# Cached attention at three rates instead of one, six page tiles loaded early, and two more half-tiles in each prompt head

## The chip, the cores and the metric

The kernel runs on one core of one Trainium2 chip. The metric is the device time of one execution in microseconds (us); three runs of the kernel before gave 2747.08, 2751.02 and 2751.05 us, with a median of 2751.02 us. One further execution was profiled: it took 2750.36 us, with a span of 2748.6 us from its first to its last instruction.

## The reference, cut to what matters

One inference step of a decoder layer over 512 prompt tokens and 8 x 8 sample tokens; the sample tokens attend to 2048 cached positions each, kept in pages.

```python
h = rms_norm(x, g_mix) @ w_in             # columns: q | k | v | forget logits | conv value | conv gate
# prompt, per head: causal softmax with a cumulative log-forget bias
s = einsum('bqhd,bkhd->bhqk', qs, k) * scale + cq[..., :, None] - c[..., None, :]
p = softmax(where(causal, s, -inf));  o = einsum('bhqk,bkhd->bqhd', p, v)
# sample, per head: the same over the cached pages and the new tokens
k_past = cache_k[l][page_table].reshape(dec_b, past, N_HEADS, HEAD_DIM)     # v_past alike
s_past = einsum('bqhd,bkhd->bhqk', q, k_past) * scale + cn[..., :, None] + r_past[..., None, :]
# both: u = value * sigmoid(gate); causal depthwise conv of width 31; LayerNorm; swish
x = x + concat([rms_norm(attn), conv_y]) @ w_out
x = x + square(relu(rms_norm(x, g_mlp) @ w_up)) @ w_down
x = x + (pe @ w_ple) * sigmoid(rms_norm(x, g_ple) @ w_ple_gate)
```

## The kernel before, in words

All 576 token rows (512 prompt, 64 sample) go through every matrix multiplication together. An f32 product is made of three products of a high and a low part, so 128 columns of `w_in` (a **column tile**) cost 16 x 3 x 2 = 96 matmuls of 128 x 288. This case is about the first stage (`phase1`, the first 800 us), which makes 40 column tiles: four of q, and then 36 in the list `order`. After that come a short drain, the output projection (`w_out`) and the MLP (`phase2`), which the change doesn't touch.

**What sets the order.** Each engine runs its instructions in the order in which the program emits them. `gemm_tile` emits a column tile in eight pieces of 12 matmuls, called halves here after the function `half()` that is called behind each. `half()` places other work between the pieces: a step of the conv work (`side`), a step of the prompt attention (`att`), and, after every second half (a **pair**), perhaps a step of the cached attention (`decode`). A counter D["credit"] grows by DEC_RATE per pair, and a decode step is emitted when it reaches 1.

**The sections of `order`.** Places 0 to 10 are c0, q4, c1, q5, c2, q6, c3, q7, c4, k0, c5 (17 column tiles, as each c is a value and a gate tile); places 11 to 15 are v0, c6, k1, c7, v1 (7 tiles); places 16 to 27 are k2, v2 to k7, v7 (12 tiles). They are called sections 1, 2 and 3 in what follows, and have 68, 28 and 48 pairs.

**The cached attention.** `decode` makes 64 steps of scores (line L847, key tiles `k`) and, four steps later, of values (L878, value tiles `v`); a step uses two key tiles and two value tiles of 512 KB. A tile is two page gathers of 256 KB, whose row numbers are read from the page table: a DMA that SyncE (SP) issues at L821. Value tiles have four buffers and key tiles five, so a value tile is asked for two steps before its use, when its buffer has come free. Each fourth step the probabilities (`dp`) are transposed into the PSUM tile `T` (L837). The generator ends with the 69th call after its start. Weights of `w_in` (`wraw`, L112) are loaded by ScalarE's queue, 256 KB for four of the 16 blocks of a tile, and split into `whi` (ScalarE) and `wlo` (VectorE).

**A shared ring of semaphores.** The DMAs of SP and of ScalarE's queue take their completion semaphores from one ring of eight, in the order in which the program was laid out. A DMA waits until the one eight places before it in that ring has landed, whichever queue issued it.

**The prompt heads.** `prompt_head(h)` is queued in `att` when tile k of head h is done, and takes one step per half: scores (`S`, L730 to L733), transposes of the probabilities into `T` (L745), v transposed (L772), values (L753), and, after a norm on VectorE (`o`, L792), the transposes of the output (L798). Heads are worked off one after the other.

Of the kernel before, what the change touches and what calls it, by code (L numbers as in the profile page):

```python
# [9 lines left out]
F32 = mybir.dt.float32  # L10
# [8 lines left out]
NR = 576  # L19
# [5 lines left out]
NPG = 16  # L25
EPS = 1e-6
SCALE = 128.0 ** -0.5
NEG = -1.0e30
DEC_RATE = 0.495
DOWN_FIRST = (3, 3, 3, 4, 5, 6, 7, 8)  # L30
DOWN_PART = 7
RING = 8
# [110 lines left out]
class Kern:  # L143
# [99 lines left out]
    def phase1(self):  # L243
        tc, nc, a = self.tc, self.nc, self.a
# [1 line left out]
        P = lambda name, bufs, **k: es.enter_context(tc.tile_pool(name=name, bufs=bufs, **k))  # L246
        Q = lambda name, bufs: pes.enter_context(tc.tile_pool(name=name, bufs=bufs, space=PSUM))
        c1, sm = P("c1", 1), P("sm", 2)
        wes, xs, st, des = ExitStack(), ExitStack(), ExitStack(), ExitStack()
        xp = xs.enter_context(tc.tile_pool(name="xp", bufs=1, side="right"))  # L250
        w1 = wes.enter_context(tc.tile_pool(name="w1", bufs=3, side="right"))
        stp = self.stp = st.enter_context(tc.tile_pool(name="stp", bufs=1, reuse_waits="tile"))
        xqp = st.enter_context(tc.tile_pool(name="xq", bufs=1, reuse_waits="tile"))
        ps_, pt_, po_, pd_, pu = Q("ps", 1), Q("pt", 1), Q("po", 1), Q("pd", 1), Q("pu", 2)
        self.c1, self.w1, self.sm = c1, w1, sm
        S_ = lambda: ps_.tile([128, 512], F32, name="S", tag="S")
# [1 line left out]
        O_ = lambda: po_.tile([128, 512], F32, name="O", tag="O")  # L258
        D_ = lambda: pd_.tile([128, 512], F32, name="D", tag="D")
        U_ = lambda: pu.tile([128, 2, 512], F32, name="U", tag="U")  # L260
# [4 lines left out]
        order = [("q", 4), ("q", 5), ("q", 6), ("q", 7), ("k", 0), ("v", 0), ("k", 1), ("v", 1)]  # L265
        order = [x for c, q in enumerate(order) for x in (("c", c), q)]
# [11 lines left out]
        self.xh, self.xl = zip(*((xp.tile([128, 2, NR], F32R, name=f"xh{j}"), xp.tile([128, 2, NR], F32R, name=f"xl{j}"))  # L278
                                 for j in range(8)))
        rb = self.rb = c1.tile([128, NR], F32, name="rb")  # L280
        raw = [xqp.tile([128, 2, NR], F32, name=f"xraw{j}") for j in range(8)]
        self.ws.dma(1)
        for i in range(2):
            nc.sync.dma_start(raw[0][:, i, :], a["x"][:, i, :])
# [64 lines left out]


        side, att, fq = deque(), deque(), deque()
        D = {"credit": 0.0, "half": 0, "dec": None, "mid": None}

        def step(q):
            while q:
# [7 lines left out]
        def half():  # L363

            D["half"] += 1
            odd = D["half"] % 2
            self.flush_later()
            if D["dec"] is None:
                step(att)
                step(fq)  # L370
                return
            step(side)
            step(att)
            if odd:
                return
            D["credit"] += DEC_RATE
            if D["credit"] >= 1.0:
                D["credit"] -= 1.0
                if next(D["dec"], self) is self and D["mid"] is None:
                    des.close()  # L380
                    D["mid"] = mes.enter_context(tc.tile_pool(name="mid", bufs=2, reuse_waits="tile"))
                    self.ple_loads(D["mid"])
                    side.append(self.finish(1, D_, O_))

        def run(gen):
            for _ in gen:
                half()

        def norm():

            fp = self.f_proj(wf, bfb)
            for j in range(4, 8):
                square(j)
                yield
            acc = raw[0][:, 0, :]
            nc.vector.tensor_tensor(acc, acc, raw[0][:, 1, :], ALU.add)
            next(fp)
            yield
            yield
            rr = self.row_rsqrt(S_, sm, raw[3][:, 0, :], acc, rb, 2048.0)  # L400
            next(rr)
            next(fp)
            yield
            for _ in rr:
                yield
            for h in range(3):
                self.evac_q(h, l0[h], l0[h])
            yield from fp
# [14 lines left out]
        st.close()  # L423
        hd, cnp = P("hd", 1, reuse_waits="tile"), P("cnp", 1, reuse_waits="tile")
        self.hd, self.cnp = hd, cnp
        self.dec = des.enter_context(tc.tile_pool(name="dec", bufs=1, reuse_waits="tile"))
        dec = D["dec"] = self.decode()
        next(dec)

        for kind, i in order:  # L430
            if kind == "c":
                for j in range(2):
                    run(self.gemm_tile(lambda u: self.evac_cin(u, j, i, cb)))
                side.append(self.conv_tile(i, cb["ue"], cb["us"]))
                if i == 7:
                    side.append(self.conv_norm())
                    side.append(self.finish(0, S_, T_))
                continue
# [18 lines left out]
        n = 0  # L457
# [260 lines left out]
    def prompt_head(self, h, hb):  # L718

        nc, hd, sm = self.nc, self.hd, self.sm  # L720
        q, k = hb["q"], hb["k"]
        o = hd.tile([128, 4, 128], F32, name="o", tag="o")
# [40 lines left out]
        scores(1)  # L763
        for _ in range(2):
            yield
        while "v" not in hb:
            for _ in range(2):
                yield
        v = hb["v"]
        t = self.S_()  # L770
# [4 lines left out]
        t = self.T_()  # L775
# [16 lines left out]
                nc.vector.tensor_tensor(o, o, rs[:, :, None].broadcast_to([128, 4, 128]), ALU.mult)  # L792
            yield
        if not self.draining:
            yield
        t = self.T_()
        for qt in range(4):
            nc.tensor.transpose(t[:, qt * 128:qt * 128 + 128], o[:, qt, :], self.ident)  # L798
# [2 lines left out]
        nc.gpsimd.dma_start(self.am[h // 2][:, h % 2, :NPR], am)  # L801


    def decode(self):


        tc, nc, a, dec, sm = self.tc, self.nc, self.a, self.dec, self.sm
        V = nc.vector.tensor_tensor
        tiles = ([], [])

        def load(i, m):

            while len(tiles[i]) < min(m, 128):
                n = len(tiles[i])
                G, c, w, j = n // 32, n // 8 % 4, n // 2 % 4, n % 2
                t = dec.tile([128, 2, 4, 128], F32, name="kv"[i], tag="kv"[i] * 2, bufs=(5, 4)[i])
                for x in range(2):
                    b, pg = (w, 2 * j + x) if i == 0 else (2 * j + x, w)
                    e = (G % 2 * 4 + b) * NPG + c * 4 + pg
                    r = nc.sync.value_load(self.pti[0:1, e:e + 1])  # L820
                    nc.sync.dma_start(t[:, x].rearrange("p h c -> p (h c)"),  # L821
                                      a["cache_kv"][bass.ds(r, 1), G // 2, :, 512 * i:512 * i + 512].rearrange("o p c -> p (o c)"))
                tiles[i].append(t)

        s = o = mu = p = None
        al, ls = {}, {}
        one = lambda name: sm.tile([128, 1], F32, name=name, tag=name)
        for n in range(68):
# [11 lines left out]
            if n < 64:  # L840
                if w == 0:
                    s = self.D_()
                    nc.tensor.matmul(s, self.selU[:, G, :], self.R[:, c * 512:c * 512 + 512], start=True, stop=False)
                for i in range(2):
                    kt = tiles[0][2 * n + i]
                    for h in range(4):
                        nc.tensor.matmul(s[32 * h:32 * h + 32, i * 256:i * 256 + 256].rearrange("p (a b) -> p a b", a=2),  # L847
                                         self.q_of(G // 2 * 4 + h, G % 2 * 4 + w), kt[:, :, h, :],
                                         start=False, stop=(w == 3 and i == 1))
                if w == 3:  # L850
                    p = dec.tile([128, 512], F32, name="dp", tag="dp")
                    mx = one("dmx")
                    nc.vector.tensor_scalar(p, s, self.cns[:, G:G + 1], None, ALU.add, ALU.max, accum_out=mx)
                    new = self.mlu[:, 0, G:G + 1]
                    if c == 0:
                        nc.vector.tensor_copy(new, mx)
                        ls[sc] = self.mlu[:, 1, G:G + 1]
                    else:
                        al[sc], ls[sc] = one("dal"), one("dls")
                        V(mx, mx, new, ALU.max)  # L860
                        V(al[sc], new, mx, ALU.subtract)
                        nc.vector.tensor_copy(new, mx)
                    nm = one("dnm")
# [1018 lines left out]
```

## Time and profile before

| | |
|---|---|
| median of three runs | 2751.02 us |
| the profiled execution | 2750.36 us, span 2748.6 us |
| TensorE (PE) busy | 2669.2 us, 97% |
| VectorE (DVE), ScalarE (ACT), GpSimd (POOL) busy | 74%, 42%, 19% |
| weights' loads into TensorE (PEld) | 2571.8 us, 94% |
| HBM read, written | 441.47 MB, 90.96 MB |
| granted TensorE clock, mean | 0.992 |

PE is the engine to follow: what it waits for adds to the end. A row of the waits names the waiting engine, its output tile and line, what it waited for, the time in total, the number of waits and the longest. "PE O L878 <- DMA v<-in_cache_kv" is TensorE's values step, waiting for a value tile to land. SP has no busy time of its own: its rows show when it issued DMAs and what held the issue up.

### The profile page before, as it was taken

The numbers are of one execution on the slowest core, as the hardware profiler recorded it, in microseconds if no ns is written. First come the engines' busy times: TensorE is split into PE (matmuls) and PEld (weight loads), VectorE is DVE, ScalarE is ACT, GpSimd is POOL, SyncE is SP. The second block draws the span as 40 slices with busy tenths as digits, with TensorE's granted clock in tenths as the row PEclk, the third lists the DMA queues.
The fourth block names the chain that finished last, engine by engine and source line by source line (L and its number), as shares of the span: only waits on it lengthen the run. The fifth ranks groups of instructions, "written<-read, shape, count | busy, mean of one in ns | idle before, by whom it ended". The sixth has DMA issues, their size and how long they took to land.

```text
span 2748.6 us, 56300 instructions
## 1 busy us (share of the span) xinstructions
PE 2669.2 (97%) x21873; PEld 2571.8 (94%) x21873; DVE 2044.5 (74%) x3553; ACT 1156.3 (42%) x1696; POOL 510.4 (19%) x906
## 2 busy tenths in 40 slices
PE   9999999999999999999999999999999999998997
PEld 8898888888889998999999999989999999998997
DVE  5576677755644447888888888899888888887676
ACT  4222223235543324444444444444444444444554
POOL 2187666721100000000000000100000000000110
PEclk9999999999999999999999999999999999999999
DMA  4688888888755454444444444666665566655675
GB/s 151 199 287 294 292 305 290 302 284 291 246 175 170 158 189 166 156 142 138 139 143 139 138 138 139 246 149 165 174 182 158 168 172 172 183 169 179 200 241 173
DMA packets 238382, 536.12 MB, mean 195 GB/s; under 512 B 25537, under 2 KB 26562, under 8 KB 238114
## 3 DMA queue, kind: packets, MB, share of 16 engines
q1 hardware_dynamic: 170978, 327.86, 37.3%
q0 software_dynamic: 33600, 143.70, 16.8%
q10 hardware_dynamic: 33536, 60.96, 6.8%
q8 instruction: 171, 2.80, 0.4%
q14 instruction: 97, 0.79, 0.1%
HBM read 441.47 MB, written 90.96 MB: 194 GB/s over the span
## 4 chain that ended last, share of the span: by engine, by line
PE 50%; issue 4%; DVE 3%; DMA 1%; ACT 1%; POOL 0%; DVEq 0%; ACTq 0%; POOLq 0%
PE P L1531 14%; PE P L1530 14%; PE P L1532 14%; PE P L1598 2%; PE P L1600 2%; PE P L1599 2%; DVE w2l L152 1%; DMA xs<-x 1%; ACT w2h L149 0%; DVE w2r L1754 0%; DVE w2r L1753 0%; DVE xs L152 0%; DVE w2r L1755 0%; DVE xs L1469 0%; DVE c L1662 0%
## 5 line engine op out<-in xcount | busy, mean ns | idle before, releaser
L1530 PE MATMUL P<-xs,w2h 128*128 128x288 f32 x3584 | 1064.6, 297 | 15.2 <-DVE c L1647 7.6
L1531 PE MATMUL P<-xs,w2h 128*128 128x288 f32 x3584 | 1064.2, 297 | 4.6 <-DVE xs L152 4.6
L1532 PE MATMUL P<-xs,w2l 128*128 128x288 f32 x3584 | 1060.9, 296 | 2.7 <-DVE w2l L152 2.7
L149 ACT ACTIVATE w2h<-w2r 128x896 fp32r<-128x896 f32 (+1 forms) x632 | 556.1, 889 | 724.4 <-PE P L1531 431.0
L152 DVE TENSOR_TENSOR w2l<-w2r,w2h 128x896 fp32r<-128x896 f32 (+1 forms) x632 | 638.2, 1012 | 218.0 <-ACT w2h L149 215.8
L1530 PEld LDWEIGHTS P<-xs,w2h 128*128 128x128 f32 x3584 | 677.1, 189 | 20.8 <-DVE c L1647 10.5
L1531 PEld LDWEIGHTS P<-xs,w2h 128*128 128x128 f32 x3584 | 677.6, 189 | 7.2 <-DVE xs L152 6.9
L1532 PEld LDWEIGHTS P<-xs,w2l 128*128 128x128 f32 x3584 | 675.4, 188 | 4.7 <-DVE w2l L152 4.4
L493 PE MATMUL U<-xh,whi 128*128 128x288 f32 x1792 | 402.5, 306 | 2.7 <-ACT whi L123 1.4
L493 PE MATMUL U<-xl,whi 128*128 128x288 f32 x1792 | 385.2, 297 | 1.7 <-DVE xl L330 1.7
L493 PE MATMUL U<-xh,wlo 128*128 128x288 f32 x1792 | 385.3, 297 | 1.4 <-DVE wlo L129 1.4
L493 PEld LDWEIGHTS U<-xh,whi 128*128 128x128 f32 x1792 | 288.6, 190 | 22.3 <-issue 14.9
L123 ACT ACTIVATE whi<-wraw 128x512 fp32r<-128x512 f32 x224 | 141.2, 630 | 392.8 <-PE U L493 228.3
L493 PEld LDWEIGHTS U<-xl,whi 128*128 128x128 f32 x1792 | 290.0, 190 | 2.9 <-DVE xl L330 2.8
L493 PEld LDWEIGHTS U<-xh,wlo 128*128 128x128 f32 x1792 | 289.5, 189 | 2.1 <-DVE wlo L129 2.1
L129 DVE TENSOR_TENSOR wlo<-wraw,whi 128x512 fp32r<-128x512 f32 x224 | 161.4, 721 | 125.8 <-ACT whi L123 121.6
L1027 DVE SCALAR_TENSOR_TENSOR y<-ue,cv,y 128x512 f32<-128x512 f32 x240 | 183.0, 763 | 5.1
L1753 DVE TENSOR_TENSOR w2r<-w2r 128x512 f32<-128x512 f32 (+1 forms) x273 | 178.1, 652 | 4.8 <-DMA w2r<-in_w_down 4.8
L1028 POOL TENSOR_SCALAR cvt<-us,cv 128x64 f32<-128x64 f32 x240 | 160.0, 667 | 22.2
L1598 PE MATMUL P<-xs,w2h 128*128 128x288 f32 x512 | 151.8, 297 | 0.6 <-ACT c L1646 0.6
L1600 PE MATMUL P<-xs,w2l 128*128 128x288 f32 x512 | 151.0, 295 | 1.1 <-DVE w2l L152 1.0
L1599 PE MATMUL P<-xs,w2h 128*128 128x288 f32 x512 | 150.8, 295 | 0.0
(383 smaller groups left out, 2765.2 us busy)
## 6 DMA issues: line engine op xcount, KB each, us to landing
k<-in_cache_kv SPq DMA_DIRECT2D x256, 256.0 KB, 4.9
v<-in_cache_kv SPq DMA_DIRECT2D x256, 256.0 KB, 4.6
w2r<-in_w_up SPq DMA_DIRECT2D x127, 512.0 KB, 4.0
w2r<-in_w_down SPq DMA_DIRECT2D x112, 512.0 KB, 4.1
wraw<-in_w_main ACTq DMA_DIRECT2D x156, 256.0 KB, 4.9
xs<-di POOLq DMA_DIRECT2D x32, 1008.0 KB, 6.1
w2r<-in_w_gate SPq DMA_DIRECT2D x60, 512.0 KB, 4.6
x<-c POOLq DMA_DIRECT2D x48, 576.0 KB, 6.3
```

What stands on the lines that cost most here:

```text
L129: self.nc.vector.tensor_tensor(lo, self.raw.pop(c), f(hi), ALU.subtract)
L149: self.nc.scalar.activation(out, in_, AF.Copy, **kw)
L152: self.nc.vector.tensor_tensor(out, in_, f(hi), ALU.subtract)
L493: self.nc.tensor.matmul(u[:, r, :HR], w, x[:, r * HR:(r + 1) * HR], start=first and n == 0, stop=last and n == 2)
L1027: nc.vector.scalar_tensor_tensor(y, ue[:, j:j + NPR], w, y, ALU.mult, ALU.add)
L1530: nc.tensor.matmul(o, hi[:, ia, :], s.hi[:, ib, :], start=(i == 0), stop=False)
L1531: nc.tensor.matmul(o, hi[:, ia, :], s.lo[:, ib, :], start=False, stop=False)
L1532: nc.tensor.matmul(o, lo[:, ia, :], s.hi[:, ib, :], start=False, stop=(i == n - 1))
L1598: nc.tensor.matmul(o, hi[:, ia, :], s.hi[:, kh, rows], start=first and kh == 0, stop=False)
L1599: nc.tensor.matmul(o, hi[:, ia, :], s.lo[:, kh, rows], start=False, stop=False)
L1600: nc.tensor.matmul(o, lo[:, ia, :], s.hi[:, kh, rows], start=False, stop=last and kh == 1)
L1753: lambda: V(w[:, :, 4:6, :], w[:, :, 0:1, :].broadcast_to([128, m, 2, 128]), w[:, :, 1:3, :], ALU.add),
```

## The change

Three edits.

1. DEC_RATE, 0.495 per pair, becomes 0.43 in section 1, 0.47 in section 2 and 0.61 in section 3.
2. The last four of the eight raw input tiles (`xraw4` to `xraw7`) get a pool of their own (`xqb`). When their squares are summed, that pool is closed and six page tiles (three keys, three values) and `dp` are placed there (`deca`), and the six are loaded at once, from within `norm`. The other two key buffers and one value buffer stay where they were (`decb`). The number of buffers is the same.
3. `prompt_head` has two changes of yields: where v was not there yet, it now waits one half at a time, and two more once v is there; and ahead of the output's transposes there are two halves and not one.

```diff
-DEC_RATE = 0.495
+DEC_RATE = (11, 0.43), (16, 0.47), (99, 0.61)
...
-            D["credit"] += DEC_RATE
+            D["credit"] += D["rate"]
...
             for j in range(4, 8):
                 square(j)
                 yield
+            xqs.close()
+            self.kv_open(des)
...
-        for kind, i in order:
+        for n, (kind, i) in enumerate(order):
+            D["rate"] = next(r for m, r in DEC_RATE if n < m)
...
-        while "v" not in hb:
+        if "v" not in hb:
+            while "v" not in hb:
+                yield
             for _ in range(2):
                 yield
...
         if not self.draining:
-            yield
+            for _ in range(2):
+                yield
...
+    KVA, KVN = 3, (5, 4)
+
+    def kv_open(self, des):
+
+        self.kvp = [des.enter_context(self.tc.tile_pool(name="deca", bufs=1, side="right", reuse_waits="tile"))]
+        self.kv = ([], [])
+        for i in range(2):
+            self.kv_load(i, self.KVA)
...
+            p = n % self.KVN[i] >= self.KVA
+            t = self.kvp[p].tile([128, 2, 4, 128], F32, name="kv"[i], tag="kv"[i] * 2, bufs=self.KVN[i] - self.KVA if p else self.KVA)
```

Where the change moves instructions, in three places. First SP's queue at the start of the cached attention. `o_logf` is the store of the prompt's forget values, `pti` the page table, `k` and `v` the page tiles. Before:

```order
L313 DMA cv<-in_convp 128x272
L315 DMA gat<-in_g_att 128x8
L576 DMA o_logf<-lf 128x40
L820 TENSOR_LOAD pti
L821 ISA
L821 DMA k<-in_cache_kv 128x512
```

And of the change, the last of the twelve early gathers and what follows:

```order
L832 DMA v<-in_cache_kv 128x512
L831 TENSOR_LOAD pti
L832 ISA
L832 DMA v<-in_cache_kv 128x512
L580 DMA o_logf<-lf 128x40
L831 TENSOR_LOAD pti
L832 ISA
L832 DMA k<-in_cache_kv 128x512
```

The store, which no gather passed before, now has twelve gathers ahead of it.

Second, TensorE's queue where the third prompt head turns v (`v` into `S` and `T`). The rows with `U` are the column tiles' matmuls; xh_202 and xl_203 are the last block of a tile. Before:

```order
L493 MATMUL U<-xh_202,whi 128x288 x2
L493 MATMUL U<-xl_203,whi 128x288 x2
L493 MATMUL U<-xh_202,wlo 128x288 x2
L772 MATMUL S<-ident,v 128x128 x4
L776 MATMUL T<-ident,v 64x128
L847 MATMUL D<-k,q_s 32x256 x8
L878 MATMUL O<-v,PT 32x128 x16
L493 MATMUL U<-xh_188,whi 128x288 x2
```

The change, where xh_193 and xl_194 are the second pair of blocks of the next tile:

```order
L497 MATMUL U<-xh_193,whi 128x288 x2
L497 MATMUL U<-xl_194,whi 128x288 x2
L497 MATMUL U<-xh_193,wlo 128x288 x2
L497 MATMUL U<-xh_193,whi 128x288 x2
L497 MATMUL U<-xl_194,whi 128x288 x2
L497 MATMUL U<-xh_193,wlo 128x288 x2
L778 MATMUL S<-ident,v 128x128 x4
L782 MATMUL T<-ident,v 64x128
L497 MATMUL U<-xh_195,whi 128x288 x2
```

The transposes of v stood right behind the tile that v comes from, and now stand two halves later.

Third, TensorE's queue in section 3 where a decode step turns its probabilities (`dp` into `T`). Before, at least one half lies between it and the prompt head's last use of `T`; the nearest case:

```order
L745 MATMUL T<-ident,p 128x128 x4
L493 MATMUL U<-xh_202,whi 128x288 x2
L493 MATMUL U<-xl_203,whi 128x288 x2
L493 MATMUL U<-xh_202,wlo 128x288 x2
L493 MATMUL U<-xh_202,whi 128x288 x2
L493 MATMUL U<-xl_203,whi 128x288 x2
L493 MATMUL U<-xh_202,wlo 128x288 x2
L960 MATMUL S<-v_s,fpT 32x128 x8
L753 MATMUL S<-vn,pT 128x128 x3
L837 MATMUL T<-ident,dp 128x128 x4
```

The change, at one of the four places of section 3 where both now fall behind the same half:

```order
L749 MATMUL T<-ident,p 128x128 x2
L734 MATMUL S<-cb,sel16R 128x384
L736 MATMUL S<-maskR,identR 128x128
L737 MATMUL S<-k,q 128x384
L854 MATMUL T<-ident,dp 128x128 x4
L860 MATMUL D<-R,selU 128x512
L864 MATMUL D<-k,q_s 32x256 x8
```

Between two uses of the one PSUM tile `T` there are now only the scores of the prompt head.

More of the change, by code (lines that the diff above doesn't have):

```diff
@@ L248, in phase1 @@
         c1, sm = P("c1", 1), P("sm", 2)
-        wes, xs, st, des = ExitStack(), ExitStack(), ExitStack(), ExitStack()
+        wes, xs, st, des, xqs = ExitStack(), ExitStack(), ExitStack(), ExitStack(), ExitStack()
         xp = xs.enter_context(tc.tile_pool(name="xp", bufs=1, side="right"))
@@ L252, in phase1 @@
         stp = self.stp = st.enter_context(tc.tile_pool(name="stp", bufs=1, reuse_waits="tile"))
-        xqp = st.enter_context(tc.tile_pool(name="xq", bufs=1, reuse_waits="tile"))
+        xqp = (st.enter_context(tc.tile_pool(name="xqa", bufs=1, reuse_waits="tile")),
+               xqs.enter_context(tc.tile_pool(name="xqb", bufs=1, side="right")))
         ps_, pt_, po_, pd_, pu = Q("ps", 1), Q("pt", 1), Q("po", 1), Q("pd", 1), Q("pu", 2)
@@ L280, in phase1 @@
         rb = self.rb = c1.tile([128, NR], F32, name="rb")
-        raw = [xqp.tile([128, 2, NR], F32, name=f"xraw{j}") for j in range(8)]
+        raw = [xqp[j // 4].tile([128, 2, NR], F32, name=f"xraw{j}") for j in range(8)]
         self.ws.dma(1)
@@ L351, in phase1 @@
         side, att, fq = deque(), deque(), deque()
-        D = {"credit": 0.0, "half": 0, "dec": None, "mid": None}
+        D = {"credit": 0.0, "half": 0, "dec": None, "mid": None, "rate": 0.0}
         def step(q):
@@ L425, in phase1 @@
         self.hd, self.cnp = hd, cnp
-        self.dec = des.enter_context(tc.tile_pool(name="dec", bufs=1, reuse_waits="tile"))
+        self.kvp.append(des.enter_context(tc.tile_pool(name="decb", bufs=1, reuse_waits="tile")))
         dec = D["dec"] = self.decode()
         next(dec)
-        for kind, i in order:
+        for n, (kind, i) in enumerate(order):
+            D["rate"] = next(r for m, r in DEC_RATE if n < m)
             if kind == "c":
@@ L801, in prompt_head, with kv_load @@
         nc.gpsimd.dma_start(self.am[h // 2][:, h % 2, :NPR], am)
+    KVA, KVN = 3, (5, 4)
[4 more added lines that the diff above has]
+            self.kv_load(i, self.KVA)
+    def kv_load(self, i, m):
+        nc, a = self.nc, self.a
+        while len(self.kv[i]) < min(m, 128):
+            n = len(self.kv[i])
+            G, c, w, j = n // 32, n // 8 % 4, n // 2 % 4, n % 2
+            p = n % self.KVN[i] >= self.KVA
+            t = self.kvp[p].tile([128, 2, 4, 128], F32, name="kv"[i], tag="kv"[i] * 2, bufs=self.KVN[i] - self.KVA if p else self.KVA)
+            for x in range(2):
+                b, pg = (w, 2 * j + x) if i == 0 else (2 * j + x, w)
+                e = (G % 2 * 4 + b) * NPG + c * 4 + pg
+                r = nc.sync.value_load(self.pti[0:1, e:e + 1])
+                nc.sync.dma_start(t[:, x].rearrange("p h c -> p (h c)"),
+                                  a["cache_kv"][bass.ds(r, 1), G // 2, :, 512 * i:512 * i + 512].rearrange("o p c -> p (o c)"))
+            self.kv[i].append(t)
     def decode(self):
-        tc, nc, a, dec, sm = self.tc, self.nc, self.a, self.dec, self.sm
+        nc, sm = self.nc, self.sm
         V = nc.vector.tensor_tensor
[L809 to L823, printed above, removed]
+        tiles, load = self.kv, self.kv_load
         s = o = mu = p = None
@@ L850, in decode @@
                 if w == 3:
-                    p = dec.tile([128, 512], F32, name="dp", tag="dp")
+                    p = self.kvp[0].tile([128, 512], F32, name="dp", tag="dp")
                     mx = one("dmx")
```

## The prediction

> **What bounds the kernel now.** I read the page's busy times first, then the waits of TensorE (PE) by stretch, then those of SyncE's (SP's) DMA queue, and last the windows with the DMA rate.
>
> ```profile
> span 2748.6 us, 56300 instructions
> PE 2669.2 (97%) x21873; PEld 2571.8 (94%) x21873; DVE 2044.5 (74%) x3553; ACT 1156.3 (42%) x1696; POOL 510.4 (19%) x906
> ```
>
> PE is idle for 79.4 us of the span. What the change can win are waits of PE in the first stage, so I cut that stage at the evictions that end the sections: q3's tile, the gate of c5, v1's tile and v7's tile.
>
> ```profile
> 90.24 0.74 DVE L702 SCALAR_TENSOR_TENSOR xraw<-U,rb 128x576 f32<-128x576 f32 x1
> 402.11 0.76 DVE L993 TENSOR_TENSOR cgate<-U,rb 128x576 f32<-128x576 f32 x1 [4.12 <-PE U L493]
> 536.25 0.76 DVE L691 TENSOR_TENSOR v<-U,rb 128x576 f32<-128x576 f32 x1 [5.02 <-PE U L493]
> 799.72 0.76 DVE L691 TENSOR_TENSOR v<-U,rb 128x576 f32<-128x576 f32 x1 [1.44 <-PE U L493]
> ```
>
> Section 1 is 90 to 402 us (312 us), section 2 is 402 to 536 (134 us), section 3 is 536 to 800 (264 us). PE's waits in the three, in that order:
>
> ```profile
> PE O L878 <- DMA v<-in_cache_kv: 11.8, 18, 2.4
> ...
> PE O L878 <- DMA v<-in_cache_kv: 4.3, 7, 0.8
> ...
> PE T L798 <- DVE o L792: 4.3, 5, 1.2
> PE S L772 <- DVE v L691: 2.6, 3, 0.9
> ```
>
> In sections 1 and 2 PE waits 11.8 + 4.3 = 16.1 us for value tiles and for hardly anything else; in section 3 it never waits for one. There it waits on the prompt heads: 4.3 us for the normed output, 2.6 us for v. So the target is at most 16.1 + 4.3 + 2.6 = 23.0 us. Why the tiles come late in one section and not in the other is in SP's queue. Issues and waits in section 1, then in 580 to 735 us (of the v gathers there one record lacks, so the moves that go with them are counted):
>
> ```profile
> L821 SPq DMA_DIRECT2D k<-in_cache_kv x136: 332/333/1631, 90.1 to 398.6; - x136
> L821 SPq DMA_DIRECT2D v<-in_cache_kv x119: 332/333/1127, 122.9 to 401.9; - x119
> SPq L821 <- DMA wraw<-in_w_main: 70.0, 40, 5.7
> SPq L821 <- PE D L847: 8.4, 5, 4.2
> SPq L821 <- PE O L878: 2.7, 7, 1.2
> ...
> L821 SPq MOVE v<-in_cache_kv x57: 29/29/37, 583.7 to 733.2; - x57
> L821 SPq DMA_DIRECT2D k<-in_cache_kv x47: 332/333/651, 580.3 to 709.1; - x47
> SPq L821 <- PE D L847: 36.6, 10, 10.2
> SPq L821 <- PE O L878: 11.0, 2, 7.1
> ```
>
> In section 1 SP hardly waits for PE to free a buffer (8.4 + 2.7 us): it is the late one. It needs (312 - 11.1) / 255 = 1.18 us per gather, 9.4 us for the eight of a step; 70.0 us of that it is held behind weight loads in the shared ring. In 580 to 735 it waits 47.6 us for PE, so its own need is (155 - 47.6) / 104 = 1.03 us, 8.3 us a step.
>
> **The pace of the cached attention.** What a decode step costs PE, and the column matmuls around it:
>
> ```profile
> 151.87 0.42 PE L493 MATMUL U<-xl,whi 128*128 128x288 f32 x2
> 152.13 0.43 PE L493 MATMUL U<-xh,wlo 128*128 128x288 f32 x2
> 152.49 1.07 PE L847 MATMUL D<-k,q_s 128*32 128x256 f32 x16
> 153.38 1.06 PE L878 MATMUL O<-v,PT 128*32 128x128 f32 x32
> 154.37 0.53 PE L493 MATMUL U<-xh,whi 128*128 128x288 f32 x2
> ```
>
> From 152.49 to 154.37 a step costs 1.88 us; with the transposes of each fourth one I take 2.0 us.
>
> Section 1: 68 pairs x 0.495 = 33.7 steps before. Without its waits PE would do one in (312 - 11.8) / 33.7 = 8.9 us, less than SP's 9.4: hence the waits. At 0.43 there are 29.2 steps, and one takes (312 - 11.8 - 4.5 x 2.0) / 29.2 = 10.0 us. SP then has 0.6 us a step to spare, and the six early tiles give it a start. I leave 0.5 us of the 11.8.
>
> Section 2: 28 pairs, 13.9 steps before, (134 - 4.3) / 13.9 = 9.3 us each; at 0.47, 13.2 steps of (134 - 4.3 - 0.7 x 2.0) / 13.2 = 9.7 us. Just above 9.4: I leave 1.0 of 4.3 us.
>
> Section 3: 48 pairs; one takes (264 - 6.9) / 48 = 5.36 us, and at 0.61 it holds 0.115 steps more, 5.59 us. That is 5.59 / 0.61 = 9.2 us a step. Against 8.3 SP still keeps up, against 9.4 it would not. The steps stop where they stopped: 29.2 + 13.2 leave 26.6 of the 69 calls, 43.6 pairs, so the 44th pair of the section; before, 69 / 0.495 = 139.4, the 140th pair of 144, which is the same one. No work is added to PE; moved steps cost nothing by themselves.
>
> The bytes of section 3 have to fit too. Its heaviest stretch holds the conv normalization's reloads:
>
> ```profile
> 580.00:640.00 60.00, 58.62 (x622) 52.14 (x615) 30.95 (x84) 24.86 (x62) 8.32 (x16) 1.00 0.95 329
> v<-in_cache_kv SPq DMA_DIRECT2D x24, 256.0 KB, 5.5
> k<-in_cache_kv SPq DMA_DIRECT2D x23, 256.0 KB, 5.5
> ```
>
> The last two columns of the first row are the DMA engines' busy share and GB/s. 47 gathers are 5.9 steps; at 0.61 they are 7.2, so 1.3 x 2.1 MB = 2.8 MB more, and 2.7 us more of PE. That asks for (329 x 60 + 2800) / 62.7 = 359 GB/s, where 329 at a share of 0.95 puts the most at 346: 2.4 us too long. The ready tiles cover a part; I leave 2.0 us of new waits (bounds 0 and 7.4, from the first rival). The Trainium skill, "DMA: Bandwidth & Descriptors", section Specifications, gives some 358 GB/s from HBM for a core; by that limit almost nothing would be left, and the sum 2 us lower. No run here has shown 358 over such a stretch.
>
> So 3.5 us of waits for tiles stay, and 16.1 - 3.5 = 12.6 us go.
>
> **The clock.** Right behind the longest wait the clock falls:
>
> ```profile
> 228.16 0.43 PE L878 MATMUL O<-v,PT 128*32 128x128 f32 x8 [2.40 <-DMA v<-in_cache_kv]
> ...
> 225.00:235.00 10.00, 7.60 (x69) 6.95 (x62) 0.86 (x2) 1.36 (x3) 0.39 (x1) 0.83 0.93 303
> 645.00:655.00 10.00, 8.11 (x77) 5.62 (x76) 4.64 (x14) 2.51 (x8) 1.31 (x3) 0.83 0.38 118
> ```
>
> A granted 0.83 over 10 us is 1.7 us lost. With the wait gone I take 1.7 us (bounds 0 and 3.4, as a second dip of the kind stands in section 3). The Trainium skill, "TensorE: Matmul & The Clock Gate", section Part 1, has the clock fall after an idle window of some 3.4 us; this wait is 2.40 us. By the page the two need not belong together, and the sum would be 1.7 us higher.
>
> **The prompt heads.** The output's transposes get a half more, 12 matmuls or 1.6 us (two take 0.26 us, from 151.87 to 152.13), and the longest of the five waits is 1.2 us: 4.3 us go. v is transposed two halves behind its eviction and never right behind it: 2.6 us go. Nobody is late next: the values, PSUM use and stores that follow all shift with them. I keep 0.4 us, so 6.5 us.
>
> In return `T` is used twice behind one half at four places. Its eviction against the scores between:
>
> ```profile
> L747 ACT ACTIVATE pT<-T 128x256 f32<-128x256 f32 (+3 forms) x24 | 10.4, 435 | 33.6 <-PE T L745 33.6
> ...
> 790.06 0.31 PE L730 MATMUL S<-cb,sel16R 128*128 128x128 f32 x1
> 790.20 0.28 PE L732 MATMUL S<-maskR,identR 128*128 128x128 f32 x1
> 790.32 0.44 PE L733 MATMUL S<-k,q 128*128 128x128 f32 x2
> ```
>
> 0.44 us of eviction stands against at least 0.70 us of scores (790.06 to 790.76), so it is covered when ACT is free; behind one whi it isn't. I take 1.0 us (bounds 0 and 4, one us at each place).
>
> **The early tiles.** They stand ahead of the store of the forget values, which held SP's first gather until 88.83 us:
>
> ```profile
> 88.83 0.34 SPq L576 DMA_DIRECT2D o_logf<-lf  x1
> 90.07 8.30 SPq L821 DMA_DIRECT2D k<-in_cache_kv  x9
> ...
> 50.00:100.00 50.00, 47.28 (x374) 43.16 (x373) 35.23 (x101) 10.02 (x19) 13.29 (x27) 1.00 0.31 98
> wraw<-in_w_main ACTq DMA_DIRECT2D x5, 256.0 KB, 3.1
> ```
>
> Twelve gathers at 8.30 / 9 = 0.92 us take 11 us of SP's queue, at a time when the DMA engines are 31% busy. The store waits for its data longer than that. Weight loads share the ring and may come later by a landing; the last row is theirs from 55 to 90 us, five in 35 us, and four are kept ahead (`RAW` of the weight stream). PE never waited for the first decode steps, so this is worth 0 by itself (bounds 0 and +8, the rival below); its worth is in SP's start.
>
> **The end of the stage.** The last head ends two halves later in the drain. There PE has the per-layer embedding's matmuls to do and the output projection's first rows behind it; I take 0 (bounds -0.5 and +2).
>
> **Sum.** -12.6 (tiles) - 1.7 (clock) - 6.5 (heads) + 1.0 (`T`) = -19.8 us. On the profiled 2750.36 us this is 2730.6; the median of the three runs is 0.7 us above it, so 2731 us, which is 0.7% faster. A measurement of this kernel can tell about 0.2%, 5.5 us, from no change.
>
> **The rivals.**
>
> *The waits move.* The bytes are the same. If section 3 gets SP's rate of section 1 (9.4 against 9.2 us a step: 26.6 x 0.2 = 5 us) and the 2.4 us of bytes, section 2 keeps its 4.3 and the clock dips elsewhere, 11.7 of the 16.1 us stay. With `T` at its bound: 2750.4 - 4.4 - 6.5 + 4.0 = 2743.5 us. For it: the 70.0 us of held issues come from the ring, which the rates leave as it is. Against: the 47.6 us in which SP waited for PE in section 3. The Trainium skill, "DMA: Bandwidth & Descriptors", section "Issuing engines are not separate DMA queues", has all queues share the same 16 DMA engines, which would speak for this rival; the share of 0.95 that three queues reach together agrees. Chance 0.16, 0.07 of it within 0.2%.
>
> The landing of SP's gathers in section 1, shortest, median and longest:
>
> ```profile
> DMA to landing us min/median/max: 2.5/4.6/7.8
> ```
>
> *Section 3 starves (slower).* There the steps come two and four halves apart, while the reloads run. If the later landing beside the reloads (5.5 us in 580 to 640, against 4.6 in section 1) stretched SP's 9.4 us by the same 1.2, a step would need 11.2 us against 9.2, and the 16 or so steps beside the reloads would wait 2.0 us each, 32 us. The rest of the sum is -19.8 - 2.0: 2750.4 - 21.8 + 32 = 2761 us. It is slower than before by more than 0.2% from a need of 9.2 + (21.8 + 5.5) / 16 = 10.9 us a step. Against: 8.3 us, measured with the reloads running. Chance 0.09.
>
> *The early tiles hold the weights.* A weight load queued behind a gather in the ring holds ScalarE's queue, and PE waits once for the 8 us between 55 and 90 us: 2739 us. For it: one ring. Against: five loads in 35 us, with four ahead. Chance 0.08.
>
> That the change doesn't move what it says is excluded by the order of the instructions.
>
> **Chances.** The forecast 0.67. Faster by over 0.2%: 0.67 + 0.09 + 0.08 = 0.84; within 0.2%: 0.07; slower: 0.09. The range reaches down to all of 16.1 + 6.9 + 3.4 us won and nothing paid (2724), and up past the first rival: 2724 to 2745 us.
>
> **What would show it.** Right: PE's wait for value tiles at 2 to 6 us in all, most of it in 580 to 680; no wait of the v transposes and under 1 us for the normed output; SP waiting for PE in section 1 by 15 us or more; no dip of the clock at 229 us. Wrong: waits for page tiles above 10 us in section 3, or weights (`whi`, `wlo`) that PE waits for between 55 and 100 us, or more than 4 us at `T` behind `pT` and `dp`.

## The result, and the profile after

The changed kernel takes 2740.48 us (median of six runs, 2734.61 to 2746.47) against 2751.81 us for the kernel before in the same comparison (six runs): a ratio of 0.9954, 95% interval 0.9939 to 0.9968. The ratio makes 12.6 us of the time before; the medians are 11.3 us apart. A second comparison, in another series, gave 0.9960 (0.9948 to 0.9973). The forecast of 2731 us was 9.5 us too low, and 2740.48 lies inside its range of 2724 to 2745. The total came out nearly right, but by luck: two of its terms were far off in opposite directions, as the experiments show.

The profiled execution took 2746.47 us, the slowest of the six, so its parts are read for where time stands, not for the size of the gain. Busy times, from the page of the changed kernel:

```profile
span 2744.7 us, 56305 instructions
PE 2670.7 (97%) x21873; PEld 2575.1 (94%) x21873; DVE 2043.5 (74%) x3553; ACT 1152.6 (42%) x1692; POOL 511.0 (19%) x906
```

The ends of the sections are read from the same four evictions as before (timeline of VectorE, changed kernel; start, duration, line):

```profile
91.89 0.74 DVE L706 SCALAR_TENSOR_TENSOR xraw<-U,rb 128x576 f32<-128x576 f32 x1
373.69 0.76 DVE L1010 TENSOR_TENSOR cgate<-U,rb 128x576 f32<-128x576 f32 x1 [0.78 <-PE U L497]
501.42 0.76 DVE L695 TENSOR_TENSOR v<-U,rb 128x576 f32<-128x576 f32 x1 [1.92 <-PE U L497]
790.76 0.76 DVE L695 TENSOR_TENSOR v<-U,rb 128x576 f32<-128x576 f32 x1 [0.99 <-PE U L497]
```

The sections last 281.8, 127.7 and 289.3 us, where they lasted 311.9, 134.1 and 263.5 us. Steps were moved from the first two into the third, so only the sum counts: 698.9 against 709.5 us, 10.6 us less. TensorE's waits in the three sections, in that order (total, number, longest):

```profile
PE S L623 <- ACT hr_v L632: 0.5, 1, 0.5
...
PE S L737 <- DVE k L695: 0.8, 1, 0.8
...
PE O L895 <- DMA v<-in_cache_kv: 11.4, 13, 2.1
PE T L854 <- ACT amt L807: 2.9, 1, 2.9
```

In sections 1 and 2 no value tile is waited for any more: 16.1 us are gone entirely. The prompt heads' waits for `o` and for `v` are gone from section 3 too. But section 3, where no value tile was waited for, now has 11.4 us of such waits. What held SP, in section 1 and then in section 3 (waits of SP's DMA queue, changed kernel):

```profile
SPq L832 <- DMA wraw<-in_w_main: 44.4, 26, 3.7
SPq L832 <- PE D L864: 38.6, 15, 8.5
...
SPq L832 <- DMA wraw<-in_w_main: 59.7, 18, 7.7
...
SPq L832 <- PE O L895: 7.5, 6, 3.7
```

In section 1 SP now waits 38.6 us for TensorE to free key buffers (8.4 us before): it is ahead. In section 3 it is the other way round. It hardly waits for buffers (7.5 us) and is held 59.7 us behind weight loads in the shared ring, 7.7 us at the longest. Before, the same row of section 3 was:

```profile
SPq L821 <- DMA wraw<-in_w_main: 13.4, 6, 5.0
```

One such hold of the changed kernel, followed through three engines (timelines of ScalarE with its queue, of SP's queue and of TensorE; the number in brackets is the idle time before the row and what ended it):

```profile
582.16 0.37 ACT L760 ACTIVATE o<-S,l 128x128 f32<-128x128 f32 x1 [3.60 <-PE S L757]
...
586.66 0.34 ACTq L112 DMA_DIRECT2D wraw<-in_w_main  x1
587.10 0.63 ACT L123 ACTIVATE whi<-wraw 128x512 fp32r<-128x512 f32 x1 [4.22 <-DVE wlo L129]
...
588.56 0.33 ACTq L112 DMA_DIRECT2D wraw<-in_w_main  x1
```

```profile
588.83 11.28 SPq L832 DMA_DIRECT2D k<-in_cache_kv  x4
600.67 3.14 SPq L832 DMA_DIRECT2D v<-in_cache_kv  x4
```

```profile
608.10 0.43 PE L895 MATMUL O<-v,PT 128*32 128x128 f32 x8 [1.13 <-ACT yl L1090]
608.83 0.43 PE L895 MATMUL O<-v,PT 128*32 128x128 f32 x8 [0.30 <-DMA v<-in_cache_kv]
610.25 0.66 PE L895 MATMUL O<-v,PT 128*32 128x128 f32 x8 [0.99 <-DMA v<-in_cache_kv]
611.50 0.65 PE L895 MATMUL O<-v,PT 128*32 128x128 f32 x8 [0.59 <-DMA v<-in_cache_kv]
```

ScalarE stands still for 3.60 us until a prompt head's values are there, and 4.22 us more until VectorE has freed the weights' buffer. Only then does it issue two weight loads. SP's four key gathers take 11.28 us to issue, 7.7 us of it in one wait for a weight load, the one issued at 588.56; it took 8.7 us to land, so the hold is made of its landing as well as of its late issue. The four value gathers follow from 600.67 us on. TensorE reads them from 608.10 on, after waits of 3.0 us over four reads. (The first bracket names `yl`, but the tile read there had landed only 0.1 us earlier, so that wait was for a tile too.) Then the clock falls (stretches of the changed kernel; the column ahead of the last two is the granted clock):

```profile
609.70:616.50 6.80, 5.66 (x34) 4.82 (x35) 0.00 (x0) 0.70 (x3) 0.00 (x0) 0.50 0.96 314
684.80:691.60 6.80, 4.65 (x35) 3.36 (x36) 2.07 (x5) 0.13 (x2) 0.69 (x2) 0.50 0.98 343
```

Twice in section 3 it stands at 0.50 for 6.8 us, each time at a value step that waits 3 to 4 us in all, and once more for 3.4 us at 701.8 us, behind the 2.9 us at `T`. The 3.4 us at 229 us are gone. Between 100 and 1000 us, every dip in the profiles of this case is 3.4 or 6.8 us long. The Trainium skill, "TensorE: Matmul & The Clock Gate", Part 1, gives a free-running window of about 3.4 us, which agrees with these lengths.

The wait at `T` (timelines of TensorE and of ScalarE, changed kernel):

```profile
697.44 0.60 PE L805 MATMUL T<-ident,o 128*128 128x128 f32 x4
...
701.33 0.67 PE L854 MATMUL T<-ident,dp 128*128 128x128 f32 x4 [2.85 <-ACT amt L807]
```

```profile
698.08 0.63 ACT L123 ACTIVATE whi<-wraw 128x512 fp32r<-128x512 f32 x1 [4.50 <-PE T L805]
698.72 1.28 ACT L1105 ACT_TABLE_LOAD   x1
700.02 0.68 ACT L1105 ACTIVATE lsg<-yl 128x576 f32<-128x576 f32 x1
700.61 0.67 ACT L807 ACTIVATE amt<-T,gat 128x512 f32<-128x512 f32 x1
```

The output's transposes and those of `dp` fell behind the same half, and the eviction between them (`amt`) stood behind a weight split, a change of ScalarE's table and a sigmoid: 2.6 us, not one `whi`.

### The profile page after: what moved, and what is told of

Same layout as the page of the kernel before. It is cut to its first block, busy times and chain, and to the rows that moved or that the text cites. A ratio compares the mean times of both kernels' runs of the same rounds, so it can differ in the third digit from the quotient of the medians.

```text
span 2744.7 us, 56305 instructions
## 1 busy us (share of the span) xinstructions
PE 2670.7 (97%) x21873; PEld 2575.1 (94%) x21873; DVE 2043.5 (74%) x3553; ACT 1152.6 (42%) x1692; POOL 511.0 (19%) x906
## 4 chain that ended last, share of the span: by engine, by line
PE 49%; issue 5%; DVE 3%; DMA 1%; ACT 1%; POOL 0%; DVEq 0%; ACTq 0%; POOLq 0%
PE P L1548 14%; PE P L1547 14%; PE P L1549 14%; PE P L1615 2%; PE P L1617 2%; PE P L1616 2%; DVE w2l L152 1%; DMA xs<-x 1%; ACT w2h L149 0%; DMA xs<-di 0%; DMA x<-c 0%; DVE w2r L1770 0%; DVE w2r L1771 0%; DVE w2r L1772 0%; DVE xs L1486 0%
```

## The experiments

### The three edits one by one, and milder rates

**Rates alone** (`p_rates`), on the kernel before:

```diff
-DEC_RATE = 0.495
+DEC_RATE = (11, 0.43), (16, 0.47), (99, 0.61)
```

> The kernel before with the three rates alone. Theory (the waits move): the value tiles' waits of sections 1 and 2 fall from 16.1 us to 1 to 4 us, but section 3 gets 9 to 13 us of them, and the clock dips behind the long ones; the prompt heads keep their 6.9 us. So only 2 to 6 us are won: ratio 0.998 to 0.9993. Rival (the prediction's sum: section 3 keeps up): section 3 has 2 to 4 us of such waits, 12 to 15 us are won, ratio 0.9945 to 0.9956.

Measured: 2730.74 us, ratio 0.9916 (0.9893 to 0.9939). Both expectations missed the time: it won 23 us, 10 more than the whole change (that one on another chip; both are repeated on one chip below). The waits are those of the rival, 3.8 us for value tiles in section 3 and none in sections 1 and 2. So section 3 does keep up by itself, as predicted, and something else in the change costs about 10 us.

**Prompt heads alone** (`p_yields`), at the one rate:

```diff
-        while "v" not in hb:
+        if "v" not in hb:
+            while "v" not in hb:
+                yield
             for _ in range(2):
                 yield
...
         if not self.draining:
-            yield
+            for _ in range(2):
+                yield
```

> The kernel before with the two further halves in a prompt head alone, at the one rate of 0.495. Theory (as in the prediction): the waits for the normed output and for v go but for 0.4 us, 6.5 us are won, T may give 1 us back; ratio 0.9976 to 0.998. Value tiles wait 15 to 17 us as before. Rival (the heads give it back at T or at the end of the stage): under 2 us won, ratio above 0.9993, with over 3 us of new waits at T.

Measured: 2750.65 us, ratio 0.9992 (0.9977 to 1.0006). Nothing that can be told from no change, and the 6.5 us of the theory (0.9976) lie just outside the interval. The rival, under 2 us with over 3 us of new waits at `T`, comes nearer. The waits of the whole stage show where they went (kernel with the heads' edit alone):

```profile
PE O L881 <- DMA v<-in_cache_kv: 20.5, 22, 2.5
PE T L840 <- ACT pT L747: 4.6, 4, 1.8
```

The 4.3 us for `o` and the 2.6 us for `v` are gone from the three sections, but value tiles stand at 20.5 us where they stood at 16.1, and `T` behind `pT` at 4.6 us, which the prediction had put at 1.0 with a bound of 4.

**Early tiles alone** (`p_early`), at the one rate and with the heads as before; the edit is the pools and `kv_load` of the change, in short:

```diff
+            xqs.close()
+            self.kv_open(des)
...
+        for i in range(2):
+            self.kv_load(i, self.KVA)
```

> The six early page tiles alone, at the one rate of 0.495 and with the prompt heads as before. Theory: SP starts with a lead of twelve gathers, but a step in section 1 asks for its tiles every 8.9 us against the 9.4 us that SP needs, so the lead is used up and the waits of section 1 (11.8 us) fall by 1 to 5 us, with a dip of the clock perhaps in another place; ratio 0.998 to 1.000. Rival (the early gathers hold the weights): PE waits up to 8 us between 55 and 100 us, ratio 1.001 to 1.003.

Measured: 2751.55 us, ratio 0.9994 (0.9978 to 1.0011), with 15.8 us of waits for value tiles in the stage. The ratio is the theory's, but its reason is not: section 1 alone has 12.4 us of these waits where it had 11.8, so they didn't fall. The start is worth nothing that shows, and no weights were waited for between 55 and 100 us.

**Milder rates** (`r57`), on the changed kernel:

```diff
-DEC_RATE = (11, 0.43), (16, 0.47), (99, 0.61)
+DEC_RATE = (11, 0.45), (16, 0.48), (99, 0.57)
```

> The changed kernel with milder rates: 0.45, 0.48 and 0.57 for 0.43, 0.47 and 0.61. Theory (section 3 is held at some 9.5 us a step by the ring, and the dips follow its long waits): a step is asked for every 9.6, 9.6 and 9.7 us in the three sections, so section 3 has 3 to 6 us of waits for value tiles instead of 11.4 us, sections 1 and 2 together 0 to 2 us, and the clock dips once less or more: 4 to 8 us faster than the changed kernel, ratio to the kernel before 0.9925 to 0.994. Rival (T and the rest of the heads took what was missing): as fast as the changed kernel, ratio 0.995 to 0.996, with the waits at T the same.

Measured: 2742.24 us, ratio 0.9950 (0.9928 to 0.9971). In section 3 the tiles' waits went as the theory said, from 11.4 to 3.4 us, but sections 1 and 2 got 5.4 us of them where 0 to 2 were expected, and the wait at `T` behind `amt` stayed, at 3.5 us. The time is that of the rival, though its interval reaches the theory's range. So this run alone doesn't decide; that the rates in section 3 are not the cause is shown by the rates alone.

### Which edit takes back what the rates win

Four kernels of one series, on one chip. The waits in the tables are those of one profiled execution of each. `r_y` is rates and heads, `r_e` rates and early tiles; the other two repeat the rates alone and the whole change.

> The three rates and the two further halves in a prompt head, without the early tiles. Theory (rates and heads get in each other's way in section 3): the rates alone won about 23 us with 3.8 us of waits for value tiles in section 3 and 2.8 us at T; with the later heads section 3 has 9 to 14 us of them and 3 to 6 us at T as in the changed kernel, so only 10 to 16 us are won: ratio 0.994 to 0.9965. Rival (the early tiles cost it): as fast as the rates alone or faster by the heads' few us, ratio 0.989 to 0.992, section 3 under 6 us.

> The three rates and the early tiles, with the prompt heads as before. Theory (rates and heads get in each other's way): like the rates alone, 3 to 6 us of waits for value tiles in section 3, none in sections 1 and 2: ratio 0.990 to 0.993. Rival (the early tiles cost it, by the buffers being in two pools): section 3 has 9 to 14 us of them, ratio 0.994 to 0.9965.

> The rates alone a second time, on the same chip as the changed kernel, since the first comparison was of different chips. If the rates alone beat the whole change: ratio 0.990 to 0.993, 5 to 12 us below the changed kernel. If that was the spread of the runs: ratio 0.994 to 0.997, within 3 us of the changed kernel.

> The whole change a second time, beside its parts. If its first comparison stands: ratio 0.994 to 0.997, and a profile with about 11 us of waits for value tiles in section 3. If the profile shown was an unlucky execution: ratio 0.990 to 0.994 and under 7 us of such waits.

| | median us | ratio | interval | value tiles' waits in section 3 | SP held by weights there |
|---|---|---|---|---|---|
| rates alone | 2732.11 | 0.9924 | 0.9906 to 0.9942 | 3.2 | 47.4 |
| rates, early tiles | 2733.85 | 0.9929 | 0.9910 to 0.9948 | 2.7 | 42.6 |
| rates, heads | 2743.31 | 0.9956 | 0.9941 to 0.9971 | 9.7 | 60.3 |
| all three | 2743.41 | 0.9960 | 0.9948 to 0.9973 | 9.5 | 63.0 |

The heads' edit costs some 10 us on the new rates; the early tiles neither cost nor bring anything that shows. Two of these profiles lie near their medians (2744.7 and 2731.8 us) and can be set side by side: stage, and from its end to the MLP's first matmul, for all three edits and then for the rates alone (stretches; the second number is the length, the third TensorE's busy time):

```profile
90.00:787.90 697.90, 682.07 (x7212) 618.16 (x7212) 447.95 (x956) 225.40 (x481) 346.90 (x627) 0.98 0.83 278
787.90:1041.59 253.69, 248.56 (x1733) 238.14 (x1732) 112.84 (x190) 86.36 (x142) 14.24 (x27) 0.99 0.51 167
```

```profile
90.04:780.47 690.43, 676.79 (x7215) 612.68 (x7215) 448.28 (x960) 230.38 (x488) 347.75 (x627) 1.00 0.86 286
780.47:1029.19 248.72, 244.21 (x1728) 234.75 (x1727) 112.14 (x186) 85.02 (x139) 14.19 (x27) 1.00 0.52 170
```

The stage is 7.5 us longer with all three. Idle time is only 2.2 us of that (15.8 against 13.6): the heads' waits that went are made up by those for value tiles and at `T`. The other 5.3 us are longer busy time, and the clock covers them: it stood at 0.50 for 23.9 us within that stage against 6.8 us. Of these, 3.4 us at 91.8 us stand in the preparation of the forget values, which the heads' edit doesn't touch; the other 13.7 us more at half speed are 6.8 us lost. The drain and the output projection are 5.0 us longer, with two dips of 3.4 us each that the rates alone lack (3.4 us lost) and head work that came later. Together this is 12.5 of the 12.9 us between the two spans.

### Which half, and the ring

The next four kernels are of another series, on another chip. `y_v` and `y_o` are the rates with one of the heads' two parts each (the loop for v; the further half ahead of the output's transposes). `wpool` is the whole change, `r_wpool` the rates alone, with the weights from the 113th load on (section 3 and the output projection) issued by GpSimd's queue, so that SP shares its ring with no weight load there:

```diff
-    AHEAD, RAW = 2, 4
+    AHEAD, RAW, SOFT = 2, 4, 112
...
-            (self.nc.sync if self.sent < self.RAW else self.nc.scalar).dma_start(t, self.srcs[self.sent])
+            (self.nc.sync if self.sent < self.RAW else self.nc.gpsimd if self.sent >= self.SOFT else self.nc.scalar).dma_start(t, self.srcs[self.sent])
```

> The three rates, and of the heads' edit only the two halves behind v (the output's transposes stay one half behind the norm). Theory (every half by which a head runs later moves its work beside the decode steps and delays the weight loads in ScalarE's queue): v's halves delay heads 1 to 7 two halves each at most, so this part makes most of the cost: 5 to 9 us of the 10 us between the rates alone (0.992) and rates with both parts (0.9956); ratio 0.994 to 0.996. Rival (the output's half makes it): ratio 0.991 to 0.993.

> The three rates, and of the heads' edit only the further half ahead of the output's transposes. Theory: one half a head, so 1 to 5 us of the 10; ratio 0.992 to 0.994, with the one wait at T behind amt (2.6 to 2.9 us) only if it comes from this part. Rival: 6 to 10 us, ratio 0.9945 to 0.996, and the waits for value tiles in section 3 at 9 to 11 us as in the whole change.

> The whole change, with the weights of section 3 loaded from GpSimd's queue in place of ScalarE's, so that SP's gathers share their ring with nobody there. Theory (SP is held by weight loads that ScalarE's queue issues late): SP's waits for weights in section 3 fall from 60 us to under 10 us, the waits of PE for value tiles from 9.5 to 11.4 us to 0 to 3 us, the dips between 600 and 700 us go; 6 to 12 us faster than the whole change: ratio 0.9915 to 0.994. Rival (the bytes in 580 to 700 us make the tiles late, whoever is first in the ring): 7 to 11 us of waits stay, ratio 0.995 to 0.997; or PE waits for the weights, which stand behind GpSimd's stores: ratio above 0.997.

> The three rates alone, with the weights of section 3 loaded from GpSimd's queue. Theory: the 3.2 to 3.8 us of waits for value tiles in section 3 and the dips of the clock beside them go, 3 to 7 us faster than the rates alone (0.992): ratio 0.9895 to 0.991, the fastest of all. Rival (GpSimd's queue brings the weights late, or the bytes decide): 0.992 or above.

| | median us | ratio | interval | value tiles' waits in section 3 | SP held by weights there |
|---|---|---|---|---|---|
| rates, v's halves | 2741.57 | 0.9944 | 0.9932 to 0.9957 | 6.4 | 51.2 |
| rates, output's half | 2732.22 | 0.9904 | 0.9889 to 0.9920 | 8.7 | 43.9 |
| whole change, weights by GpSimd | 2727.84 | 0.9895 | 0.9879 to 0.9912 | 0 | 0 |
| rates, weights by GpSimd | 2728.12 | 0.9892 | 0.9874 to 0.9910 | 0 | 0 |

The two halves behind v make the cost, as their theory said; the one ahead of the output's transposes makes none, and `y_o` came out below both of its ranges. But `y_o` has 8.7 us of waits for value tiles, which its rival had expected, and yet the lower time: its heads' waits are gone, its idle time in the stage is 13.8 us, as with the rates alone, and the clock never dipped there. So the sum of these waits is not the cost; whether they come in clusters that bring the clock down is part of it (the last section has what the records show of that).

With the weights out of the ring section 3 reads like this (waits of SP's queue, then of TensorE, whole change with weights by GpSimd):

```profile
SPq L832 <- PE D L864: 25.7, 11, 5.1
SPq L832 <- PE O L895: 14.6, 7, 8.4
```

```profile
PE T L854 <- ACT amt L807: 3.8, 1, 3.8
PE S L189 <- DVE ldg L183: 0.7, 1, 0.7
```

SP waits for TensorE again, 40.3 us, and TensorE for no tile at all. The bytes are the same, and a gather takes longer to land than in the whole change (median 6.4 and 6.7 us for v and k against 4.7 and 4.9), so it was where the weight loads stand, in SP's ring and behind ScalarE's other work, and not the memory. The whole change gains 16 to 18 us by this (0.9895 against 0.9954 and 0.9960 in the other series), more than the 6 to 12 us of the theory. The wait at `T` stays. Both kernels with weights by GpSimd beat before and after, at 0.989; against the rates alone (0.9916 and 0.9924 in the other series) the intervals still touch.

The pair also shows what the heads' edit is worth when no gather is late. Stage and what follows it to the MLP, for the whole change and then for the rates alone, both with weights by GpSimd:

```profile
90.25:772.70 682.45, 674.78 (x7211) 613.61 (x7211) 447.08 (x956) 223.91 (x481) 374.45 (x680) 0.99 0.85 285
772.70:1027.04 254.34, 249.02 (x1733) 238.23 (x1732) 111.36 (x190) 85.29 (x142) 45.81 (x86) 0.99 0.51 167
```

```profile
90.70:778.40 687.70, 675.48 (x7216) 613.59 (x7217) 449.22 (x959) 229.17 (x488) 378.46 (x680) 1.00 0.85 287
778.40:1025.24 246.84, 241.89 (x1728) 232.03 (x1728) 110.69 (x186) 84.03 (x139) 45.77 (x86) 1.00 0.52 172
```

The heads win 5.3 us in the stage, 4.6 us of it idle time, and lose 7.5 us behind it: 3.4 us by two dips of the clock that the other lacks, about 1 us by the few matmuls more that stand there, and some 3 us that these rows don't explain. The times of the two kernels agree: 0.9895 and 0.9892.

## Why the prediction was right or wrong, point by point

- **The total** was in the range by luck, because errors offset each other. The rates won 21 to 23 us where their terms (12.6 + 1.7) made 14.3; the heads cost some 10 us on these rates where 6.5 were to be won.
- **Tiles in sections 1 and 2**: right. 16.1 us went (1.5 had been left), and SP's wait for TensorE in section 1 rose from 8.4 to 38.6 us, as the step "10.0 us against SP's 9.4" wanted.
- **Section 3 keeps up (9.2 against 8.3 us a step)**: right for the rates alone (3.2 and 3.8 us of waits, 2.0 forecast), wrong for the whole change (11.4 and 9.5 us). The step that failed is SP's own need of 8.3 us. It had been measured where SP waited 47.6 us for TensorE, and there it met few weight loads that had not landed (13.4 us of such holds in section 3 before). SP asked to go faster is held by the weights: 47.4 us in section 3 with the rates alone, 59.7 and 63.0 us with the whole change. By the prediction's own working, in its stretch of 580 to 735 us, a gather of the changed kernel needs (155 - 4.5) / 110 = 1.37 us and not 1.03, 10.9 us a step, against the 9.2 us in which a step is asked for. The heads' part in this goes by way of ScalarE: ScalarE's wait for a head's values (`o`) in section 3 is 47.8 us in the changed kernel and 29.4 with the rates alone. Part of that is an effect and not a cause, as ScalarE waits longer where TensorE does: with the weights by GpSimd it is 31.7 us with the heads' edit and 28.8 without. The sign that the prediction itself named as wrong, over 10 us of tile waits in section 3, came true in the first profile (11.4 us) and nearly in the second (9.5 us).
- **"The waits move"**, the first rival, described section 3 of the changed kernel, but by its mechanism only in part: it had put the cause in the rates and in the bytes. Neither holds as the cause, since the rates alone don't do it and moving the weight loads ends it with the same bytes. What it had right is the ring, which the rates leave as it is.
- **The clock**: the dip at 229 us went, as forecast. That waits in section 3 would bring more of them was not priced: the stage has 17.0 and 23.9 us at half speed in the two profiles of the changed kernel where it had 6.8, so instead of 1.7 us won, 5.1 and 8.5 us more are lost, the 1.7 us at 91.8 us among the latter.
- **The heads, -6.5 us**: all waits for `o` and `v` went from section 3, as said. "Nobody is late next" is the step that failed. Late next were the value tiles, `T`, and the drain, and on the new rates the edit costs some 10 us.
- **`T`, +1.0 (bounds 0 and 4)**: one wait of 2.9 us in the changed kernel, 4.6 us over four with the heads alone. The cover by 0.70 us of scores was priced against `pT`; the long wait came behind `amt`, with a table load of 1.28 us ahead of it.
- **Early tiles, 0**: right (0.9994 alone; 0.9929 against 0.9924 on the rates).
- **The end of the stage, 0 (bounds -0.5 and +2)**: too low. From v7's tile to the MLP it took 252.4 and 253.7 us in the two profiles of the changed kernel, 250.2 before and 248.7 with the rates alone; the bound was passed in both.

**Still open.** `wpool` takes the weights out of the ring and out of ScalarE's order in one; which of the two helped more was not tried. How the heads' edit makes 10 us of it is read from profiles (tile waits, dips, the drain); that it does so only while ScalarE loads the weights is shown by the two pairs of kernels. The rates alone shorten the stage by 19.0 us, of which 14.5 are idle time; the 4.5 us of busy time that went with it, at the same 6.8 us of dips, are not explained. Nor was `y_o` with weights by GpSimd run, which by these numbers might be the best.

## What to carry to other kernels

A queue's own speed, read while it waits for its consumer, says nothing of what it does when it is asked for more: look at what else holds it, here a ring shared with another engine's loads, and take the rate from the section where it is late. An edit that removes a wait of the bottleneck by moving work later has to be priced on what shares its queues (ScalarE's weight loads, one PSUM tile) and on where the moved work ends up. Try the edits of a change one by one: here one of three brought everything, one nothing, and one took half of it back.

## What the runs showed of the hardware that had not been expected

The prediction took 346 GB/s as the most that the core's DMA engines move, from 329 at a share of 0.95. The rates alone with weights by GpSimd, over 15 us (share and GB/s at the end):

```profile
685.00:700.00 15.00, 13.93 (x181) 12.12 (x185) 5.48 (x8) 9.05 (x15) 3.76 (x7) 1.00 1.03 383
```

383 GB/s, so the rate worked out from a share was no ceiling: 383 at 1.03 is 372 at a full share, where 329 at 0.95 had made 346. Why the two differ isn't shown. The Trainium skill, "HBM Reference", Specifications, has a core that streams alone measure up to about 425 GB/s, above the 358 that it gives as a core's share; 383 agrees with that sentence and not with 358 as a limit.

A half-speed clock needed no single long wait. In the steps with the dips at 609.7 and 684.8 us the longest single wait was 1.1 and 1.3 us, four waits within 6 us; the longest wait for a tile in that profile, 2.1 us until 654.95, had no dip behind it. Where the waits fall seems to decide. Within a profile the dips start whole multiples of 3.413 us apart: in the changed kernel 22, 5 and 36 of them lead from 609.7 to 684.8, 701.8 and 824.7 us. Cut each profile from 100 to 1000 us into stretches of 3.413 us on that grid. All 36 dips of the fourteen profiles follow a stretch in which TensorE was idle for 1.48 us or more. Outside a dip, every stretch with more than 1.86 us of idle time is followed by one; in between it goes either way.

The grid cut the 2.1 us wait in two, with 1.5 us of idle time in one stretch and 0.9 us in the next. The waits of 0.8 and 0.7 us at the first weights of the output projection fell into one stretch before (1.48 us, and a dip at 902 us), and into two with the rates alone, second run (no dip). This is read from the records and was not tried by an experiment. It means that a profile's dips, and with them some us of its time, hang in part on where the grid lay in that execution.
